# Odd chunks with their halves swapped: 64x64 products over four quarters of the array, and a block-diagonal serial product

## The chip, the cores and the metric

The kernel runs on one core of one Trainium2 chip. The metric is device time in microseconds of one execution of the whole program. The core has a matrix engine (TensorE, PE in the profile; its weight loads are listed as PEld), three engines for elementwise work (VectorE, DVE; ScalarE, ACT; GpSimd, POOL) and SyncE (SP), whose queue issues most of the transfers. TensorE writes its results to PSUM, in banks of 128 partitions by 512 float32; VectorE and ScalarE read them from there.

## What is computed

A hybrid decoder block over 16 meta tokens and 1024 tokens of width 1024: a half-step SwiGLU, then a mixer with two branches, (A) a chunked gated DeltaNet and (B) an RWKV-7 time mixing, then a second half-step SwiGLU. All is float32. The change is in branch B, whose recurrence the reference gives a token at a time:

```python
def _rwkv7_scan(r, w, k, v, a_vec, b_vec):
    def step(state, inp):
        r_t, w_t, k_t, v_t, a_t, b_t = inp
        sa = jnp.einsum('bhvk,bhk->bhv', state, a_t)
        state = state * w_t[:, :, None, :] + sa[..., None] * b_t[:, :, None, :] \
            + v_t[..., None] * k_t[:, :, None, :]
        return state, jnp.einsum('bhvk,bhk->bhv', state, r_t)
    ...
```

B has 16 heads of 64 channels. The kernel takes chunks of 64 tokens, and writes what a chunk does to the state as products of 64x64 matrices.

## The kernel before

The program has three stages: `ffn1`, `middle` and `ffn2`. `middle` works in two segments of 512 tokens (the first has the 16 meta tokens beside them) and, in each, through eight iterations; an iteration handles one head of A and two heads of B, which lie in partitions 0 to 63 and 64 to 127 (`HS`). So there are 16 iterations, with `NCB` = 8 chunks of B in each.

An iteration is made of actions: `new_b` and `new_a` (nine projections of the input with `gates`, 24 matmuls of 128x128 for each block of columns, tile `pp`, and the operands from them), `operands` (products within a chunk, tiles `grb`, `bkt`, `vp`), `inverses` (the triangular inverses in blocks of 32: operands go to DRAM and come back as `Ub`, VectorE solves them, the results go out and return as `Xc` and `Y`), `merge_blocks` (inverses of 64 from those of 32, tiles `iv`), `chains` with `transitions` in front of it (products of the chunks that need the inverse, then the serial part over the chunks), `gates` and `finish`. In the regular case iteration `it` runs `merge_blocks chains`, then `new_b new_a operands inverses` of the next iteration, then `gates finish`. That is the order in which the program is written; the order in which each engine gets its instructions is made by the framework's planner, which goes by priority in the written order, by readiness and by its own estimate of times. The timeline of the trace therefore shows projections of the next iteration between the steps of `chains`.

A 64x64 product takes rows (the partitions of its operands) and columns (the partitions of its result) of the array, a half of each: four quarters. `rows 0 to columns 0` and `1 to 1` are the diagonal ones. In `operands` and `transitions` the 64x64 products go chunk by chunk and half by half:

- `vbp` in `new_b`, L984: 16 products off the diagonal (from half `hp` to half `hx`), into `Vs`.
- `bkt`, L1150: both kinds of `BK` transposed, one to the same half and one to the other: all four quarters, two PSUM banks.
- `vp`, L1167: first `pa` (diagonal) with `pv` (off it), then `pr` with `pk`, both off it. ScalarE copies them to `at`, `vka`, `yb`, `vbk`.
- `transitions`, L1319: six runs of 16 products on the diagonal: `xp` twice (the inverse times `at`, and times `vka`), `mp`, `np`, `rp`, `yp`, each in a bank of its own of the pool `ch`, which has two.
- `chains`, L1397: for each chunk the serial product `b`, two 64x64 matmuls (`mt` times the state `SBs`), then VectorE's update of the state, L1398. After every second chunk comes a chunk of A (tiles `p`, `pq`).

The trace has two records for each float32 matmul, so a run of 16 products is 32 records, and a `b` of one chunk is four. The pool `ch` serves `merge_blocks`, `transitions`, `chains` and `finish`; the pool `mx` serves `new_b` and `operands`, with two banks in the first segment and three in the second.

## Time and profile before

| | |
|---|---|
| Time, median of 3 runs | 3205.22 us (3203.47 to 3205.88) |
| The profiled execution | 3201.6 us, span 3199.8 us |
| TensorE busy | 3064.5 us (96%), 25654 matmul records |
| VectorE, ScalarE, GpSimd busy | 1950.8, 1330.9 and 457.8 us |
| Mean granted TensorE clock | 0.98 |
| first start of `grb` and last start of `bq` in `middle` | 840.6 and 2411.2 us |

The page of the profile gives busy time by engine, the same in 40 slices, the chain of work that ended last, and groups of instructions by line. The span leaves out 1.8 us around it. Matmuls overlap, so the sum of their lengths is not the time that TensorE needs for them; what counts is how far apart they start. A row of the timeline is a stretch of like instructions: start, length from the first start to the last end, engine, line, operation, what it writes and reads, and the count. A bracket tells of idle time before it and what ended it.

### The profile page before, as it was taken

The page shows a single profiled execution, that of the slowest core. Times are in us where ns is not written, and L with a number is a line of the kernel's source. Part 1 is how long each engine was busy: PE and PEld are TensorE (multiplying, and loading weights), DVE is VectorE, ACT ScalarE, POOL GpSimd, SP SyncE. Part 2 cuts the span into 40 slices and gives each one's busy share as a digit, 9 for nine tenths or more (in the row PEclk, how much of TensorE's full clock was granted, in tenths as well). Part 3 has the DMA queues.
Part 4 walks back from the last instruction along what each step waited for, and adds up shares of the span by engine and source line. Part 5 has one row for each costly group of instructions (what it writes and reads, how often), then busy time and mean ns, then how long its engine had stood idle before and what let it go on. Part 6 is the DMA issues. An engine that isn't in the chain of part 4 may idle for free.

```text
span 3199.8 us, 61487 instructions
## 1 busy us (share of the span) xinstructions
PE 3064.5 (96%) x25654; PEld 2578.9 (81%) x25654; DVE 1950.8 (61%) x3628; ACT 1330.9 (42%) x2196; POOL 457.8 (14%) x588
## 2 busy tenths in 40 slices
PE   5999999999899999999999999999999899999998
PEld 5999998998878887888777777777776688887886
DVE  7554444346666776667667777667766755554335
ACT  4222222125545555455565555555544422222114
POOL 4222220000000000000011000011001433322000
PEclk8999999999999999999999999999999999999999
DMA  2222224234122322222332232322255132224323
GB/s 92 93 94 80 80 83 160 77 95 142 60 66 65 81 61 70 69 72 73 92 92 70 73 82 66 79 76 77 76 163 174 64 99 91 80 79 147 109 79 110
DMA packets 256566, 287.16 MB, mean 90 GB/s; under 512 B 168272, under 2 KB 174416, under 8 KB 256288
## 3 DMA queue, kind: packets, MB, share of 16 engines
q1 hardware_dynamic: 252048, 271.42, 28.5%
q0 software_dynamic: 2512, 8.65, 0.7%
q8 instruction: 201, 3.29, 0.4%
q10 hardware_dynamic: 1728, 3.16, 0.3%
q14 instruction: 77, 0.63, 0.1%
HBM read 232.70 MB, written 50.47 MB: 88 GB/s over the span
## 4 chain that ended last, share of the span: by engine, by line
PE 62%; DVE 5%; ACT 3%; DMA 2%; issue 2%; POOL 1%; SPq 0%; DVEq 0%; POOLq 0%; ACTq 0%
PE pp L259 24%; PE pg L422 12%; PE pd L259 7%; PE pwo L259 3%; PE cs L921 2%; PE vp L1167 1%; DMA Xc<-scX 1%; PE b L1397 1%; PE gra L1121 1%; PE grb L1080 1%; PE p L1376 1%; PE bkt L1150 1%; PE pq L1385 1%; DVE w L155 1%; PE iv L1278 1%
## 5 line engine op out<-in xcount | busy, mean ns | idle before, releaser
L259 PE MATMUL pp<-uk,w 128*128 128x264 f32 (+1 forms) x4824 | 987.8, 353 | 3.8 <-DVE gg L1437 3.8
L259 PEld LDWEIGHTS pp<-uk,w 128*128 128x128 f32 x4824 | 751.7, 192 | 122.5 <-issue 21.2
L154 ACT ACTIVATE w<-wraw 128x1024 fp32r<-128x1024 f32 (+2 forms) x332 | 328.5, 990 | 731.7 <-PE pd L259 289.9
L259 PE MATMUL pd<-hd,w 128*128 128x512 f32 (+1 forms) x2640 | 501.0, 352 | 13.2 <-DVE w L155 6.0
L259 PEld LDWEIGHTS pd<-hd,w 128*128 128x128 f32 x2640 | 430.2, 190 | 82.9 <-DVE w L155 8.1
L422 PE MATMUL pg<-bt,w 128*128 128x260 f32 (+1 forms) x2772 | 458.0, 322 | 22.5 <-ACT bt L154 9.4
L422 PEld LDWEIGHTS pg<-bt,w 128*128 128x128 f32 x2772 | 401.5, 190 | 67.6 <-ACT bt L154 10.0
L428 DVE TENSOR_TENSOR c<-c,pg 128x520 f32<-128x520 f32 (+1 forms) x308 | 207.9, 688 | 366.7 <-PE pg L422 301.6
L155 DVE TENSOR_TENSOR w<-wraw,w 128x1024 fp32r<-128x1024 f32 (+2 forms) x332 | 381.9, 1150 | 78.8 <-ACT w L154 72.9
L422 PE MATMUL pg<-b,w 128*128 128x260 f32 (+1 forms) x2376 | 392.3, 321 | 9.2 <-POOL b L155 5.0
L422 PEld LDWEIGHTS pg<-b,w 128*128 128x128 f32 x2376 | 345.7, 190 | 44.2 <-POOL b L155 5.4
L392 POOL TENSOR_TENSOR wrx<-wrx 128x512 f32<-128x512 f32 x44 | 66.6, 1513 | 575.6 <-DVE w22b L155 308.4
L154 ACT ACTIVATE w<-wrx 128x1024 fp32r<-128x1024 f32 (+1 forms) x66 | 60.2, 912 | 180.4 <-PE pg L422 170.0
L1245 DVE TENSOR_TENSOR Xb<-Xb,tb 115x126 f32<-115x126 f32 (+22 forms) x496 | 126.0, 254 | 12.3
L1243 DVE TENSOR_TENSOR tb<-Ub,Xb 115x126 f32<-115x126 f32 (+22 forms) x496 | 125.1, 252 | 11.9 <-DMA Ub<-scr 0.2
L1043 DVE SCALAR_TENSOR_TENSOR acc<-xr,pk,acc 128x528 f32<-128x528 f32 (+1 forms) x144 | 108.7, 755 | 30.7 <-ACT acc L1039 28.6
L539 DVE SCALAR_TENSOR_TENSOR h<-pd,h 128x528 f32<-128x528 f32 (+1 forms) x64 | 44.5, 697 | 119.6 <-PE pd L259 119.6
L539 DVE SCALAR_TENSOR_TENSOR hh<-pd,hh 128x512 f32<-128x512 f32 x64 | 44.1, 689 | 109.9 <-PE pd L259 106.5
L259 PE MATMUL pwo<-uk,w 128*128 128x512 f32 x384 | 99.1, 409 | 6.2 <-ACT rg L922 2.7
L259 PEld LDWEIGHTS pwo<-uk,w 128*128 128x128 f32 x384 | 71.6, 191 | 25.7 <-ACT rg L922 3.5
L839 ACT ACTIVATE sh<-pp,pk 128x528 f32<-128x528 f32 (+1 forms) x54 | 37.2, 690 | 126.9 <-PE pp L259 115.8
L154 ACT ACTIVATE hd<-hr 128x1040 fp32r<-128x1040 f32 (+1 forms) x44 | 45.4, 1061 | 79.1 <-DMA hr<-hid 52.6
(382 smaller groups left out, 3980.2 us busy)
## 6 DMA issues: line engine op xcount, KB each, us to landing
wraw<-in_win SPq DMA_DIRECT2D x150, 512.0 KB
wraw<-in_wgu SPq DMA_DIRECT2D x44, 512.0 KB
wrx<-in_wgu SPq DMA_DIRECT2D x44, 512.0 KB
wraw<-in_wdn SPq DMA_DIRECT2D x48, 320.0 KB
wraw<-in_wdn SPq DMA_DIRECT2D x32, 384.0 KB
hid<-c SPq DMA_DIRECT2D x44, 260.0 KB
hr<-hid SPq DMA_DIRECT2D x22, 520.0 KB
hid<-c SPq DMA_DIRECT2D x44, 256.0 KB
```

The costliest lines, as they stand in the source:

```text
L154: g.nc.scalar.activation(hi, src, AF.Copy)
L155: (eng or g.nc.vector).tensor_tensor(lo, src, hi.bitcast(F32), op=ALU.subtract)
L259: g.nc.tensor.matmul(ps, lhsT=l, rhs=r, start=i == 0, stop=i == n - 1)
L392: nc.gpsimd.tensor_tensor(a22, a21, a22, op=ALU.add)
L422: nc.tensor.matmul(ps[:, c0 : c0 + cn], lhsT=l[:, x, k, :], rhs=r[:, k, y, c0 : c0 + cn], start=i == 0, stop=i == 3 * HK - 1)
L428: nc.vector.tensor_tensor(o, x, y, op=ALU.add)
L539: nc.vector.scalar_tensor_tensor(hv, pd, 0.5, hv, op0=ALU.mult, op1=ALU.add)
L839: nc.scalar.activation(sh[:, 1 : 1 + n], ps, AF.Identity, scale=g.V("mu", i))
L921: nc.tensor.matmul(ps[:, :cn], lhsT=lhsT, rhs=sq[:, c0 : c0 + cn], start=True, stop=True)
L1043: nc.vector.scalar_tensor_tensor(acc[:, :n], xr[:, tap : tap + n], V("convw", ct * 4 + tap), acc[:, :n], op0=ALU.mult, op1=ALU.add)
L1243: nc.vector.tensor_tensor(tv, U[:, i, i + 1 :].unsqueeze(2).to_broadcast([npt, nt, ncc]), X[:, i, 0:ncc].unsqueeze(1).to_broadcast([npt, n ...
L1245: nc.vector.tensor_tensor(X[:, i + 1 :, 0:ncc], X[:, i + 1 :, 0:ncc], tv, op=ALU.add)
```

## The change

For odd chunks the two heads swap halves on the side of the tokens: `tok(i, h)` is the half in which head `h` of chunk `i` has its tokens, `key(i, h)` the other one. A product of an even chunk on diagonal quarters then lies off the diagonal for an odd chunk, and the reverse. A new function `run` issues one or more kinds of products one after another; results of diagonal quarters go to one PSUM bank and those of the others to a second, so that a kind has its even chunks in one bank and its odd ones in the other, four chunks (256 columns) each, and each copy out of PSUM becomes two of half the width. The two kinds of one call share the two banks.

- `new_b`: `vbp` goes through `run`.
- `operands`: `pa` with `pr` in one call, `pk` (`vb`) in another. `pv` moves to `transitions` (`va`). `LT` and `BKt` are held by diagonal and off-diagonal, no longer by kind.
- `inverse_inputs`: the four stores of `LT` become eight, even and odd chunks apart.
- `transitions`: four calls: the inverse times `at` (`px`) with `va`; the inverse times `vka`; `mp` with `rp`; `np` with `yp`. The multiply of `vbk` by `gam` goes from GpSimd to VectorE.
- `g.mt` is a tile of 128x128 for each chunk, allocated once and cleared once, with the two heads' matrices as its diagonal blocks; `b` is one matmul with it.

```diff
--- before.py
+++ after.py
@@ -30,7 +30,7 @@
 NT = NCB + NCA
 NBLK = 4 * NT
 HS = (slice(0, 64), slice(64, 128))
-HX = ((HS[0], HS[1]), (HS[1], HS[0]))
+EO = (slice(0, NCB, 2), slice(1, NCB, 2))
 CDEC = math.exp(-0.5)
 EPS = 1e-6
 NJ = 8
@@ -720,7 +720,9 @@
         g.Y = [ms.tile([P, NT, P], F32, name=f"Y{i}") for i in range(2)]
         g.XA = ms.tile([CB, NCA, 2, 2, 16], F32, name="XA")
         g.Ub = ms.tile([115, 32, 32], F32, name="Ub")
-        for t in (*g.Y, g.XA, g.Ub):
+
+        g.mt = ms.tile([P, NCB, P], F32, name="mt")
+        for t in (*g.Y, g.XA, g.Ub, g.mt):
             nc.gpsimd.memset(t, 0.0)
 
         g.unit = ms.tile([P, CB], F32, name="unit")
@@ -924,6 +926,38 @@
         nc.scalar.activation(out[:, :n], out[:, :n], AF.Exp, scale=-0.5)
     else:
         nc.scalar.activation(out[:, :n], out[:, :n], AF.Exp, scale=-0.5, bias=bias)
+
+
+def tok(i, h):
+
+    return h ^ (i & 1)
+
+
+def key(i, h):
+
+    return 1 - tok(i, h)
+
+
+def run(g, pool, name, *kinds):
+
+
+    ps, out, used = {}, [], [0, 0]
+    for f in kinds:
+        ds = [f(i, 0)[2] ^ f(i, 0)[3] for i in range(2)]
+        at = []
+        for d in ds:
+            if d not in ps:
+                ps[d] = pool.tile([P, 512], F32, name=name, tag=pool.name)
+            at.append(used[d])
+            used[d] += NCB // 2 * CB
+        for i in range(NCB):
+            e, c0 = ds[i & 1], at[i & 1] + i // 2 * CB
+            for h in range(2):
+                l, r, src, dst = f(i, h)
+                assert src ^ dst == e
+                g.nc.tensor.matmul(ps[e][HS[dst], c0 : c0 + CB], lhsT=l, rhs=r, start=True, stop=True)
+        out.append([(ch3(ps[d][:, c0 : c0 + NCB // 2 * CB], CB), cs) for d, c0, cs in zip(ds, at, EO)])
+    return out
 
 
 def new_b(g, it):
@@ -978,12 +1012,9 @@
 
     Vs = q.Vs = st.tile([P, NCB, CB], F32, name="Vs", tag="Vs", bufs=2)
     k = shifted(g, c, 40 + j, 8 + j, "kB")
-    ps = g.mx.tile([P, 512], F32, name="vbp", tag="mx")
-    for i in range(NCB):
-        for hp, hx in HX:
-            nc.tensor.matmul(ps[hx, i * CB : (i + 1) * CB], lhsT=v[hp, off + i * CB : off + (i + 1) * CB],
-                             rhs=g.C("cmat")[hp, hp], start=True, stop=True)
-    nc.scalar.activation(Vs, ch3(ps, CB), AF.Copy)
+    for ps, cs in run(g, g.mx, "vbp", lambda i, h: (v[HS[h], off + i * CB : off + (i + 1) * CB],
+                                                    g.C("cmat")[HS[h], HS[h]], h, key(i, h)))[0]:
+        nc.scalar.activation(Vs[:, cs], ps, AF.Copy)
     if meta:
         ps = g.mx.tile([P, 512], F32, name="vbm", tag="mx")
         nc.tensor.matmul(ps[:16, 0:P], lhsT=v[:, 0:16], rhs=g.C("cmat"), start=True, stop=True)
@@ -1071,16 +1102,17 @@
 
 
 
+
     LT = q.LT = st.tile([P, NCB, 2, P], F32, name="LT", tag="LT", bufs=2)
     for c4 in range(0, NCB, 4):
         ps = [g.mx.tile([P, 512], F32, name="grb", tag="mx") for _ in range(2)]
         for i in range(4):
-            for y in range(2):
-                for hp in HX:
-                    nc.tensor.matmul(ps[y][hp[y], i * P : (i + 1) * P], lhsT=BK[hp[0], c4 + i, y],
-                                     rhs=AR[hp[0], c4 + i].rearrange("p a b -> p (a b)"), start=True, stop=True)
-        for y in range(2):
-            nc.vector.tensor_tensor(LT[:, c4 : c4 + 4, y], ch3(ps[y], P),
+            for d in range(2):
+                for h in range(2):
+                    nc.tensor.matmul(ps[d][HS[h ^ d], i * P : (i + 1) * P], lhsT=BK[HS[h], c4 + i, d ^ (i & 1)],
+                                     rhs=AR[HS[h], c4 + i].rearrange("p a b -> p (a b)"), start=True, stop=True)
+        for d in range(2):
+            nc.vector.tensor_tensor(LT[:, c4 : c4 + 4, d], ch3(ps[d], P),
                                     g.C("mB").unsqueeze(1).to_broadcast([P, 4, P]), op=ALU.mult)
     if meta:
         nc.vector.tensor_copy(g.bkpm[0:64, 0, :], g.bkm[0:64, :])
@@ -1142,40 +1174,36 @@
     inverse_inputs(g, q)
 
     BKt = q.BKt = st.tile([P, NCB, 2, CB], F32, name="BKt", tag="BKt", bufs=2)
-    at = q.at = st.tile([P, NCB, CB], F32, name="at", tag="at")
+    ident = g.C("ident")
     ps = [g.mx.tile([P, 512], F32, name="bkt", tag="mx") for _ in range(2)]
     for i in range(NCB):
-        for y in range(2):
-            for hp in HX:
-                nc.tensor.matmul(ps[y][hp[y], i * CB : (i + 1) * CB], lhsT=BK[hp[0], i, y],
-                                 rhs=g.C("ident")[hp[0], hp[0]], start=True, stop=True)
-    for y in range(2):
-        nc.scalar.activation(BKt[:, :, y], ch3(ps[y], CB), AF.Copy)
+        for d in range(2):
+            for h in range(2):
+                nc.tensor.matmul(ps[d][HS[h ^ d], i * CB : (i + 1) * CB], lhsT=BK[HS[h], i, d ^ (i & 1)],
+                                 rhs=ident[HS[h], HS[h]], start=True, stop=True)
+    for d in range(2):
+        nc.scalar.activation(BKt[:, :, d], ch3(ps[d], CB), AF.Copy)
 
     Vs = q.Vs
-    vka, vbk = (st.tile([P, NCB, CB], F32, name=x, tag=x) for x in ("vka", "vbk"))
-    q.vka, q.vbk = vka, vbk
+    at = q.at = st.tile([P, NCB, CB], F32, name="at", tag="at")
+    vbk = q.vbk = st.tile([P, NCB, CB], F32, name="vbk", tag="vbk")
     yb = q.yb = st.tile([P, FULL], F32, name="yb", tag="yb", bufs=2)
 
-    def kind(name, *ops):
-
-        ps = [g.mx.tile([P, 512], F32, name=name, tag="mx") for _ in ops]
-        for i in range(NCB):
-            for p, op in zip(ps, ops):
-                for hp, hx in HX:
-                    l, r = op(i, hp, hx)
-                    nc.tensor.matmul(p[hp, i * CB : (i + 1) * CB], lhsT=l, rhs=r, start=True, stop=True)
-        return ps
-
-    ident = g.C("ident")
-    pa, pv = kind("vp", lambda i, hp, hx: (AR[hp, i, 0, :], ident[hp, hp]),
-                  lambda i, hp, hx: (LT[hx, i, 1, :CB], Vs[hx, i]))
-    nc.scalar.activation(at, ch3(pa, CB), AF.Copy)
-    nc.scalar.activation(vka, ch3(pv, CB), AF.Copy)
-    pr, pk = kind("vp", lambda i, hp, hx: (Vs[hx, i], LT[hx, i, 1, CB:]),
-                  lambda i, hp, hx: (BKt[hx, i, 1], Vs[hx, i]))
-    nc.scalar.activation(yb, pr, AF.Copy)
-    nc.scalar.activation(vbk, ch3(pk, CB), AF.Copy)
+    def vr(i, h):
+        k = key(i, h)
+        return Vs[HS[k], i], LT[HS[k], i, 1 - (i & 1), CB:], k, h
+
+    def vb(i, h):
+        k = key(i, h)
+        return BKt[HS[k], i, 1 - (i & 1)], Vs[HS[k], i], k, h
+
+    pa, pr = run(g, g.mx, "vp", lambda i, h: (AR[HS[h], i, 0, :], ident[HS[h], HS[h]], h, tok(i, h)), vr)
+    for ps, cs in pa:
+        nc.scalar.activation(at[:, cs], ps, AF.Copy)
+    for ps, cs in pr:
+        nc.scalar.activation(ch3(yb, CB)[:, cs], ps, AF.Copy)
+    for ps, cs in run(g, g.mx, "vp", vb)[0]:
+        nc.scalar.activation(vbk[:, cs], ps, AF.Copy)
     if meta:
         btm = q.btm = st.tile([64, P], F32, name="btm", tag="btm")
         ps = g.mx.tile([P, 512], F32, name="btp", tag="mx")
@@ -1207,7 +1235,8 @@
     sv = scr.rearrange("(t b) r c -> b r t c", b=4)
     for b in range(4):
         sl, lo = slice(32 * b, 32 * b + 32), 32 * (b % 2)
-        nc.sync.dma_start(sv[b][:, 0:NCB], q.LT[sl, :, 0, lo : lo + 32])
+        for e, cs in enumerate(EO):
+            nc.sync.dma_start(sv[b][:, cs], q.LT[sl, cs, e, lo : lo + 32])
     for b in range(4):
         sl = slice(32 * b, 32 * b + 32)
         nc.sync.dma_start(sv[b][:, NCB:], q.UA[sl, :, 32 * b : 32 * b + 32])
@@ -1274,7 +1303,7 @@
     ps = g.ch.tile([P, 512], F32, name="iv1", tag="ch")
     for t in range(NT):
         for o in (0, 64):
-            u12 = LT[o : o + 32, t, 0, 32:64] if t < NCB else UA[o : o + 32, t - NCB, o + 32 : o + 64]
+            u12 = LT[o : o + 32, t, t & 1, 32:64] if t < NCB else UA[o : o + 32, t - NCB, o + 32 : o + 64]
             nc.tensor.matmul(ps[o + 32 : o + 64, t * 32 : t * 32 + 32], lhsT=u12, rhs=nat(Xc[o : o + 32, t]),
                              start=True, stop=True)
     for o in (0, 64):
@@ -1308,30 +1337,47 @@
 
     nc, st = g.nc, g.st
     Y = g.Y[q.it % 2]
-    AR, LT, BKt, vbk, yb = q.AR, q.LT, q.BKt, q.vbk, q.yb
-    flat = lambda t: t.rearrange("p c m -> p (c m)")
-
-    def product(pool, name, op):
-        ps = getattr(g, pool).tile([P, 512], F32, name=name, tag=pool)
-        for i in range(NCB):
-            for hp in HS:
-                l, r = op(i, hp)
-                nc.tensor.matmul(ps[hp, i * CB : (i + 1) * CB], lhsT=l, rhs=r, start=True, stop=True)
-        return ps
-
-    xa, xv = (st.tile([P, NCB, CB], F32, name=x, tag=x) for x in ("xa", "xv"))
-    nc.scalar.activation(flat(xa), product("ch", "xp", lambda i, hp: (Y[hp, i, hp], q.at[hp, i])), AF.Copy)
-    nc.scalar.activation(flat(xv), product("ch", "xp", lambda i, hp: (Y[hp, i, hp], q.vka[hp, i])), AF.Copy)
-    mt = q.mt = st.tile([P, NCB, CB], F32, name="mt", tag="mt")
-    ps = product("ch", "mp", lambda i, hp: (xa[hp, i], BKt[hp, i, 0]))
-    nc.vector.tensor_tensor(mt, ch3(ps, CB), g.unit.unsqueeze(1).to_broadcast([P, NCB, CB]), op=ALU.add)
-    ps = product("ch", "np", lambda i, hp: (BKt[hp, i, 0], xv[hp, i]))
-    nc.vector.tensor_tensor(vbk, ch3(ps, CB), vbk, op=ALU.add)
-    nc.gpsimd.tensor_tensor(vbk, vbk, q.gam.unsqueeze(2).to_broadcast([P, NCB, CB]), op=ALU.mult)
-    ps = product("ch", "rp", lambda i, hp: (xa[hp, i], LT[hp, i, 0, CB:]))
-    nc.vector.tensor_tensor(AR[:, :, 1, :], ch3(ps, CB), AR[:, :, 1, :], op=ALU.add)
-    ps = product("ch", "yp", lambda i, hp: (xv[hp, i], LT[hp, i, 0, CB:]))
-    nc.vector.tensor_tensor(yb, ps, yb, op=ALU.add)
+    AR, LT, BKt, Vs, vbk, yb = q.AR, q.LT, q.BKt, q.Vs, q.vbk, ch3(q.yb, CB)
+    xa, xv, vka = (st.tile([P, NCB, CB], F32, name=x, tag=x) for x in ("xa", "xv", "vka"))
+
+    def solved(r):
+        def f(i, h):
+            t = tok(i, h)
+            return Y[HS[t], i, HS[t]], r[HS[t], i], t, t
+        return f
+
+    def by_tok(l, r):
+        def f(i, h):
+            t = tok(i, h)
+            return l(HS[t], i), r(HS[t], i), t, h
+        return f
+
+    def va(i, h):
+        k = key(i, h)
+        return LT[HS[k], i, 1 - (i & 1), :CB], Vs[HS[k], i], k, 1 - k
+
+    px, pv = run(g, g.ch, "xp", solved(q.at), va)
+    for ps, cs in pv:
+        nc.scalar.activation(vka[:, cs], ps, AF.Copy)
+    for ps, cs in px:
+        nc.scalar.activation(xa[:, cs], ps, AF.Copy)
+    for ps, cs in run(g, g.ch, "xp", solved(vka))[0]:
+        nc.scalar.activation(xv[:, cs], ps, AF.Copy)
+    bt = lambda r, i: BKt[r, i, i & 1]
+    br = lambda r, i: LT[r, i, i & 1, CB:]
+    pm, pr = run(g, g.ch, "mp", by_tok(lambda r, i: xa[r, i], bt), by_tok(lambda r, i: xa[r, i], br))
+    for ps, cs in pm:
+        for hp in HS:
+            nc.vector.tensor_tensor(g.mt[hp, cs, hp], ps[hp], g.unit[hp].unsqueeze(1).to_broadcast([CB, NCB // 2, CB]),
+                                    op=ALU.add)
+    for ps, cs in pr:
+        nc.vector.tensor_tensor(AR[:, cs, 1, :], ps, AR[:, cs, 1, :], op=ALU.add)
+    pn, py = run(g, g.ch, "np", by_tok(bt, lambda r, i: xv[r, i]), by_tok(lambda r, i: xv[r, i], br))
+    for ps, cs in pn:
+        nc.vector.tensor_tensor(vbk[:, cs], ps, vbk[:, cs], op=ALU.add)
+    nc.vector.tensor_tensor(vbk, vbk, q.gam.unsqueeze(2).to_broadcast([P, NCB, CB]), op=ALU.mult)
+    for ps, cs in py:
+        nc.vector.tensor_tensor(yb[:, cs], ps, yb[:, cs], op=ALU.add)
 
 
 def chains(g, q):
@@ -1393,8 +1439,7 @@
     nc.gpsimd.tensor_copy(SBs[:, 0], SB)
     for i in range(NCB):
         ps = pt("b1")
-        for hp in HS:
-            nc.tensor.matmul(ps[hp, :CB], lhsT=q.mt[hp, i], rhs=SBs[hp, i], start=True, stop=True)
+        nc.tensor.matmul(ps[:, :CB], lhsT=g.mt[:, i], rhs=SBs[:, i], start=True, stop=True)
         nc.vector.scalar_tensor_tensor(SBs[:, i + 1], ps[:, :CB], q.gam[:, i : i + 1], q.vbk[:, i],
                                        op0=ALU.mult, op1=ALU.add)
         if i % 2 == 0:
```

## Prediction

> **What bounds the kernel now.** I read the page first: busy shares, the slices, the chain that ended last.
>
> ```profile
> span 3199.8 us, 61487 instructions
> PE 3064.5 (96%) x25654; PEld 2578.9 (81%) x25654; DVE 1950.8 (61%) x3628; ACT 1330.9 (42%) x2196; POOL 457.8 (14%) x588
> PE   5999999999899999999999999999999899999998
> PE 62%; DVE 5%; ACT 3%; DMA 2%; issue 2%; POOL 1%; SPq 0%; DVEq 0%; POOLq 0%; ACTq 0%
> ```
>
> TensorE is busy 96% of the span and in every slice but the first; the chain runs mostly over it. The change lies in the middle stage, so the next view is the table of stretches: one iteration of the first segment, one of the second.
>
> ```profile
> 1044.00:1144.00 100.00, 94.65 (x1067) 79.56 (x1065) 66.76 (x162) 50.03 (x97) 8.40 (x25) 0.98 0.27 72
> 2049.00:2141.00 92.00, 89.51 (x956) 68.63 (x952) 66.37 (x151) 49.94 (x89) 8.72 (x18) 1.00 0.29 77
> ```
>
> Columns: length, then busy time of PE, PEld, DVE, ACT and POOL with instruction counts, granted clock, DMA. TensorE fills 94.7 of 100 and 89.5 of 92 us; VectorE has a quarter free, ScalarE half. The list of TensorE's waits tells what the rest is.
>
> ```profile
> PE iv L1278 <- DMA Xc<-scX: 14.4, 7, 2.8
> PE vbp L984 <- DVE vB L840: 7.2, 3, 4.9
> PE vp L1167 <- ACT BKt L1153: 2.6, 8, 0.6
> PE np L1319 <- ACT xv L1324: 1.4, 5, 0.3
> ```
>
> (Total, times, longest.) The largest wait that comes again is 14.4 us in seven iterations, for the inverses' blocks that come back by DMA. The products that the change touches hardly wait. So the middle lasts as long as TensorE's instructions take one after another, and what is to be priced is TensorE time.
>
> **A product on two quarters and on four.** A 64x64 product is one matmul in the program and two records in the trace. From the timeline, one iteration's products on the diagonal quarters alone:
>
> ```profile
> 1930.17 1.15 PE L1319 MATMUL xp<-vka,Y 64*64 64x64 f32 x32
> 1931.20 1.15 PE L1319 MATMUL mp<-BKt,xa 64*64 64x64 f32 x32
> 1932.63 1.15 PE L1319 MATMUL np<-xv,BKt 64*64 64x64 f32 x32 [0.28 <-ACT xv L1324]
> 1934.77 1.15 PE L1319 MATMUL rp<-LT,xa 64*64 64x64 f32 x32
> 1935.75 1.10 PE L1319 MATMUL yp<-LT,xv 64*64 64x64 f32 x32
> 1936.71 0.33 PE L1397 MATMUL b<-SBs,mt 64*64 64x64 f32 x4
> ```
>
> One record lasts 0.22, so 32 records start within 1.15 - 0.22 = 0.93 us: 29 ns each. For four quarters there are two places. The transposes `bkt` use all four (the stretch from 1257, those instructions alone), and so do the first two kinds of `vp` where they run well:
>
> ```profile
> 1257.00:1259.00 2.00, 1.44 (x64) 1.30 (x64) 0.37 (x1) 1.00 0.18 26
> 1874.86 0.22 PE L1167 MATMUL vp<-Vs,LT 64*64 64x64 f32 x1
> 1874.86 0.22 PE L1167 MATMUL vp<-ck,AR 64*64 64x64 f32 x1
> 1874.87 0.22 PE L1167 MATMUL vp<-Vs,LT 64*64 64x64 f32 x1
> 1874.87 0.22 PE L1167 MATMUL vp<-ck,AR 64*64 64x64 f32 x1
> 1874.92 0.22 PE L1167 MATMUL vp<-Vs,LT 64*64 64x64 f32 x1
> ```
>
> 64 records of `bkt` start within 1.44 - 0.22 = 1.22 us, 19 ns each. In the steady part four start within 0.01 us and the next four 0.06 us later, 15 ns each. A quarter takes one record in 58 ns whatever the others do; `bkt` loses 0.29 us over its steady rate (64 x 14.5 ns = 0.93) because the second of its two PSUM banks comes free later, and its records on that bank trail.
>
> Here a rule speaks against the change. The Trainium skill, page "TensorE: Matmul & The Clock Gate", section "Part 3: Packing small matmuls — row/col tiling", says that a weight load overlaps running matmuls only where it targets other rows of the array. By it, two quarters that share rows would take turns, four would give no more than two, and the products would gain nothing; the rows of `bkt` and `vp` above disagree.
>
> **The change part by part, per iteration (16 of them).** There are eleven products of 16 matmuls before and after; what moves is which quarters meet in one run. From the index functions in the diff: `vbp`, `pa` with `pr`, `pk`, `mp` with `rp`, `np` with `yp` alternate over four quarters. But `solved` reads rows `t` and writes rows `t`: `px` and the second `xp` stay on the diagonal, and `va`, emitted after `px`, stays off it. Those three keep the rate of two quarters. In us:
> - before: `vbp` 0.93; `pa` with `pv` 1.22 (as `bkt`); `pr` with `pk`, both off the diagonal, 1.86; six of `transitions` 5.58. Sum 9.59.
> - after, at 19 ns a record: `vbp` 0.61, `pa`+`pr` 1.22, `pk` 0.61, `px`+`va` 1.86, `xv` 0.93, `mp`+`rp` 1.22, `np`+`yp` 1.22. Sum 7.67, 1.9 less.
> - after, at 15 ns and with `va` starting under the end of `px`: 0.51 + 0.98 + 0.51 + 1.72 + 0.93 + 0.98 + 0.98 = 6.61, 3.0 less.
>
> I take 2.4, half way, since some runs will find their second bank late and others not: 38 us over 16 iterations. Low end: if every run has its even chunks first and the odd ones after, two quarters work at a time throughout and only `pa`, which loses its partner, changes: -0.6 an iteration, a loss of 10 us. High end 49.
>
> **The serial product.** `b` goes from two 64x64 matmuls to one 128x128, 128 times. Timeline, both segments:
>
> ```profile
> 1109.05 1.36 PE L259 MATMUL pp<-uk,w 128*128 128x264 f32 x9
> 1116.92 0.39 PE L259 MATMUL pp<-uk,w 128*128 128x264 f32 x1
> 1127.13 0.89 PE L259 MATMUL pp<-uk,w 128*128 128x264 f32 x5
> 1127.86 0.38 PE L1376 MATMUL p<-SA,kq 128*128 128x128 f32 x2
> 1128.00 0.73 PE L259 MATMUL pp<-uk,w 128*128 128x264 f32 x4
> 1636.08 1.03 PE L895 MATMUL tkp<-ck,c 128*128 128x16 f32 x8 [1.22 <-DVE c L881]
> 1940.35 0.48 PE L259 MATMUL pp<-uk,w 128*128 128x512 f32 x1
> 1940.76 0.33 PE L1397 MATMUL b<-SBs,mt 64*64 64x64 f32 x4
> 1941.02 0.97 PE L259 MATMUL pp<-uk,w 128*128 128x512 f32 x3
> ```
>
> A projection matmul of 512 columns adds (0.97 - 0.48) / 2 = 0.24. From the `pp` ahead of `b` to the `pp` behind it are 0.67, so `b` between projections costs 0.43. A full-array product: `p` is followed by the next `pp` after 0.14; the whole stretch from 1127.13 to 1128.00 is 0.87, less five short projections of 0.12 ((1.36 - 0.39) / 8) it is 0.27, the first projection's start behind `b` included; `tkp`, full array with only 16 columns, needs (1.03 - 0.26) / 7 = 0.11 a record, 0.22 a product. I take 0.22, the one in the middle: 0.21 saved, 128 times, 27 us. Ends: 0.43 - 0.14 = 0.29 gives 37; a `b` that follows a product and not a projection (1936.71 to 1936.97 is 0.26) saves only 0.04, 5 us if all were such. The step's own delay grows from 0.33 to about 0.11 + 0.26 = 0.37; VectorE already waits for `b`, and projections stand between the steps, so the 0.04 x 128 = 5 us are covered; without that cover they come on top.
>
> **What is added.**
>
> ```profile
> L1124 DVE TENSOR_TENSOR UA<-gra,E 128x256 f32<-128x256 f32 x32 | 13.5, 421 | 6.4 <-PE gra L1121 5.8
> L1327 DVE TENSOR_TENSOR mt<-mp,unit 128x512 f32<-128x512 f32 x16 | 11.0, 687 | 12.5 <-PE mp L1319 12.5
> L1330 POOL TENSOR_TENSOR vbk<-vbk,gam 128x512 f32<-128x512 f32 x16 | 19.0, 1187 | 159.7 <-DVE vbk L1329 159.7
> L1323 ACT ACTIVATE xa<-xp 128x512 f32<-128x512 f32 x16 | 9.6, 597 | 3.5 <-PE xp L1319 3.4
> ```
>
> VectorE: four operations of 0.69 become ten halves of 0.42, and the multiply by `gam` (0.69 here, 1.19 on POOL) joins: 4.9 against 2.8, 2.1 us more. ScalarE: seven copies of 0.60 become fourteen of perhaps 0.42, 1.7 more. Both hide under TensorE, since these engines have 25 and 42 us an iteration free; uncovered they are 34 and 27 us in all. The added clear of `mt` on POOL is one of 1024 columns before the stage's first product and hides under the last projections of `ffn1`.
>
> Each run now holds both `ch` banks until all its halves are read, where before one bank was filled while the other was emptied. So TensorE waits four times an iteration for 2 to 6 such operations, 0.8 to 2.5 us, with the chain's `b` and `p` behind it on the same queue. The cover is projections: 9 x 24 an iteration at 0.24, which the planner places into waits that it sees. I count two more interruptions of the projections an iteration at 0.43 - 0.22 = 0.21 each: 7 us lost. Uncovered, four waits of 1.5 us are 96 us.
>
> SP issues eight stores of `LT` for four:
>
> ```profile
> 1871.27 1.80 SPq L1210 DMA_DIRECT2D scr<-LT  x4
> 1873.18 2.65 SPq L1213 DMA_DIRECT2D scr<-UA  x4
> ```
>
> That is 1.8 us more, ahead of the stores of `UA`, the loads of `Ub` and the next weights on that queue. The weights are fetched one tile ahead and hide it. The inverses are later by up to 1.8 us; the second segment shows no wait for them and has some slack, the first waits 2 us in each of seven iterations already, so there this delay and the shorter `vp` work turn into waiting: about 1 us x 7 = 7 us lost, 7 x 3.5 = 25 at most.
>
> **Sum.** 38 + 27 - 7 - 7 = 51. The profiled execution took 3201.6 us, so 3151; the median of the runs shown is 3.6 higher, and on its scale I forecast 3155.
>
> **Rivals.**
> 1. The products gain nothing: the banks come free so far apart that the halves run two quarters at a time (`bkt`'s late bank speaks for it, its 19 ns against it), or quarters that share rows take turns. Left are 27 - 14 = 13 us, with the low end of the products near zero: 3192; with half of the products' gain 3175.
> 2. Everything fits: 49 + 37 and no losses: 3119. For it: VectorE and ScalarE have room. Against it: the wait for `Xc` is there already.
> 3. Slower: the runs that hold both `ch` banks leave TensorE idle. From 51 / 16 = 3.2 us idle an iteration on, the gain is gone; four uncovered waits of 1.5 us give 3155 + 16 x 6 = 3251. For it: the first run of `transitions` now stands ahead of a copy, a product, a copy again. Against it: `np` waited for `xv` 1.4 us in all.
> 4. The change does not do what it says and its costs meet its gains: no change, 3205.
>
> **How the numbers follow.** Forecast (3130 to 3172) 0.60; rival 1 0.20, three quarters of it faster by over 0.2%; rival 2 0.10; rival 3 0.07; rival 4 0.03. 0.2% is 6.4 us, about what a measurement of this kernel can tell from no change. Faster: 0.60 + 0.15 + 0.10 + a little of the rest = 0.86; same 0.07; slower 0.07. The range from 3117 to 3192 takes in most of rivals 1 and 2 and leaves out rival 3.
>
> **What the profile will show.** Right: `vbp`, `mp` with `rp` and `np` with `yp` as runs of 32 and 64 records that start within 0.5 to 0.6 and 1.0 to 1.2 us; `b` with two records, 128x128, and 0.2 us between the projections around it; the iteration of the second segment at 88 to 89 us; `px` and `xv` still at 0.93. Wrong: waits of TensorE for `mt`, `vbk`, `xa` or `xv` of over a microsecond, `Xc` waits above 30 us in all, or VectorE above 80% with TensorE below 93%. What would upset the forecast most is a new order from the planner in which the projections are used up before the runs need them.

## The result and the profile after

| kernel | median, us | runs | ratio to before, 95% interval |
|---|---|---|---|
| before | 3204.34 | 4 | |
| changed | 3176.49 (3172.09 to 3179.78) | 4 | 0.9914, 0.9897 to 0.9931 |
| changed, second time (below) | 3178.90 (3173.06 to 3181.99) | 5 | 0.9928, 0.9916 to 0.9941 |

The change gains 28 us where 50 were forecast; 3176 lies 4 us above the forecast's likeliest case (3130 to 3172) and inside its whole range (3117 to 3192). The profiled execution took 3179.03 us, 22.6 less than the one before, and the readings below are of these two.

Page of the changed kernel: span, busy shares, chain by engine. Then the table of stretches, one iteration of the second segment from `iv` to `iv` (length, busy time of PE, PEld, DVE, ACT, POOL with counts, granted clock, DMA). Then TensorE's waits (total, times, longest).

```profile
span 3177.2 us, 61363 instructions
PE 3048.8 (96%) x25398; PEld 2563.7 (81%) x25398; DVE 1972.4 (62%) x3740; ACT 1336.5 (42%) x2308; POOL 436.2 (14%) x573
PE 62%; DVE 5%; ACT 3%; DMA 3%; issue 1%; POOL 0%; SPq 0%; DVEq 0%; POOLq 0%; ACTq 0%
```

```profile
2080.20:2171.70 91.50, 91.03 (x946) 69.65 (x945) 69.77 (x161) 50.23 (x95) 7.78 (x18) 1.00 0.30 79
```

```profile
PE iv L1307 <- DMA Xc<-scX: 15.8, 7, 3.0
PE np L958 <- DVE AR L1374: 6.0, 3, 3.5
```

TensorE is the bound as before: 96%, at a granted clock of 1.00 in this stretch. The mean of four iterations here went from 91.35 to 90.10 us; in the first segment from 103.3 to 102.5. The wait for `Xc` grew by 1.4 us, and three waits of `np` for VectorE are new. From the first `grb` to the last `bq` the middle takes 1560.5 us, 10 less than before; the other 12 us show behind the last `bq`, mostly because only 225 of the 384 records of the output projection (`pwo`) are left there, where 272 were. That is work moved ahead and not work saved, so the gain is read from the products and not from the stages.

To see where TensorE's time went, I give each of its matmuls in the trace the time from its start to the start of the next one (an idle stretch goes to the matmul ahead of it) and add up by product, us over the whole run. All kernels of the next section stand in the same table. "chain" is `p` and `pq`; "transitions" had six products before and has seven since, `va` having left `vp`.

| product | before | b alone | products alone | changed | two quarters | both edits | va first |
|---|---|---|---|---|---|---|---|
| vbp | 18.1 | 18.1 | 10.7 | 10.7 | 16.9 | 10.4 | 10.4 |
| vp | 64.8 | 65.1 | 49.6 | 50.3 | 54.6 | 44.4 | 49.1 |
| transitions | 104.5 | 100.3 | 103.0 | 103.4 | 106.4 | 100.9 | 84.4 |
| b | 31.4 | 31.0 | 29.1 | 32.6 | 31.9 | 26.5 | 28.5 |
| chain | 77.7 | 73.5 | 82.7 | 79.4 | 77.5 | 80.5 | 79.0 |
| grb | 51.5 | 50.1 | 55.8 | 56.9 | 55.0 | 54.0 | 53.1 |
| pp | 968.9 | 964.6 | 975.5 | 971.6 | 978.2 | 973.8 | 991.0 |
| all other | 1856.3 | 1862.9 | 1844.6 | 1845.7 | 1840.2 | 1845.1 | 1845.8 |
| sum | 3173.2 | 3165.6 | 3151.0 | 3150.6 | 3160.7 | 3135.6 | 3141.3 |

The first three rows are the forecast's "products": 187.4 before, 164.4 after, so 23 us and not 38. `b` costs as much as before. Three runs of products in the changed kernel, from TensorE's timeline (start, length to the last end, count; a row is a group of like instructions, and rows in between are left out):

```profile
1882.73 0.69 PE L958 MATMUL vbp<-ck,vB 64*64 64x64 f32 x32
1914.56 0.63 PE L958 MATMUL mp<-BKt,xa 64*64 64x64 f32 x16
1915.02 0.63 PE L958 MATMUL mp<-LT,xa 64*64 64x64 f32 x14
1915.48 0.68 PE L958 MATMUL mp<-BKt,xa 64*64 64x64 f32 x16
1916.00 0.63 PE L958 MATMUL mp<-LT,xa 64*64 64x64 f32 x18
1919.14 0.73 PE L958 MATMUL np<-xv,BKt 64*64 64x64 f32 x31
1919.71 0.66 PE L958 MATMUL np<-LT,xv 64*64 64x64 f32 x30
```

`vbp`: 32 records start within 0.69 - 0.22 = 0.47 us where two quarters took 0.93. `np` with `yp`: 64 start within 1.0 us here, and within 1.26 in seven of the 16 iterations. But `mp` with `rp` runs the even halves of both products first and then the odd ones, 1.9 us: two quarters at a time. And the chain's steps stand among other products than before:

```profile
1934.66 0.43 PE L1112 MATMUL grb<-AR,BK 64*64 64x128 f32 x2
1935.02 0.43 PE L1442 MATMUL b<-SBs,mt 128*128 128x64 f32 x2
1935.38 0.87 PE L1112 MATMUL grb<-AR,BK 64*64 64x128 f32 x12
```

The next iteration's `grb` now lies between the steps; before, it began after `bq` in the second segment. The planner made a new order: 24 of the 128 `b` stand between two projections, where 45 stood.

### The profile page after: what moved, and what is told of

Same layout as the page of the kernel before. It is cut to its first block, busy times and chain, and to the rows that moved or that the text cites. A ratio compares the mean times of both kernels' runs of the same rounds, so it can differ in the third digit from the quotient of the medians.

```text
span 3177.2 us, 61363 instructions
## 1 busy us (share of the span) xinstructions
PE 3048.8 (96%) x25398; PEld 2563.7 (81%) x25398; DVE 1972.4 (62%) x3740; ACT 1336.5 (42%) x2308; POOL 436.2 (14%) x573
## 4 chain that ended last, share of the span: by engine, by line
PE 62%; DVE 5%; ACT 3%; DMA 3%; issue 1%; POOL 0%; SPq 0%; DVEq 0%; POOLq 0%; ACTq 0%
PE pp L259 23%; PE pg L422 12%; PE pd L259 7%; PE pwo L259 2%; PE cs L923 2%; PE grb L1112 1%; DMA Xc<-scX 1%; PE b L1442 1%; PE xp L958 1%; PE vp L958 1%; PE gra L1153 1%; PE bkt L1182 1%; PE np L958 1%; PE pq L1431 1%; DVE w L155 1%
## 5 line engine op out<-in xcount | busy, mean ns | idle before, releaser
L154 ACT ACTIVATE hd<-hr 128x1040 fp32r<-128x1040 f32 (+1 forms) x44 | 45.4, 1061 | 79.4 <-DMA hr<-hid 52.9
```

Source lines behind the costliest of these rows:

```text
L154: g.nc.scalar.activation(hi, src, AF.Copy)
```

## The experiments

Ratios are to the kernel before, run beside each on the same chip; the experiments ran on three chips, so they are compared with each other by these ratios. The diffs are shortened: `...` and comments stand for what is left out.

**The two parts apart.** The products and `b` each alone. For `b` alone:

```diff
+        g.mt = ms.tile([P, NCB, P], F32, name="mt")      # cleared once
-    nc.vector.tensor_tensor(mt, ch3(ps, CB), g.unit..., op=ALU.add)
+    for hp in HS:
+        nc.vector.tensor_tensor(g.mt[hp, :, hp], ch3(ps, CB)[hp], g.unit[hp]..., op=ALU.add)
-        for hp in HS:
-            nc.tensor.matmul(ps[hp, :CB], lhsT=q.mt[hp, i], rhs=SBs[hp, i], start=True, stop=True)
+        nc.tensor.matmul(ps[:, :CB], lhsT=g.mt[:, i], rhs=SBs[:, i], start=True, stop=True)
```

> The kernel before with the serial product alone changed: mt is one 128x128 block-diagonal tile, b one matmul, the products stay as they were. Theory A: half of the 128 products b wait for ScalarE's copy of pq, which reads the PSUM bank that this b writes; the row of the forecast (0.43 us between projections) was one of these, and its cost is the wait. Such a b stays at 0.40; the other half, which follows the product p, goes from 0.36 to 0.17 (both from the timelines of before and after). That is 64 x 0.19 = 12 us, so 3192, a ratio of 0.996. Theory B, the forecast's: every b saves 0.21, 27 us: 3177, 0.9916. Theory C: the planner gives it all back: within 3 us of before.

Measured 3184.13 (3182.35 to 3195.34), ratio 0.9957 (0.9943 to 0.9972): 14 us, near theory A's 12. The profiled execution was one of the two slowest of six, 3194.05, so its column in the table shows less of the gain. TensorE's timeline of this kernel:

```profile
1937.51 0.48 PE L259 MATMUL pp<-uk,w 128*128 128x512 f32 x1
1937.90 0.43 PE L1398 MATMUL b<-SBs,mt 128*128 128x64 f32 x2
1938.14 0.94 PE L259 MATMUL pp<-uk,w 128*128 128x512 f32 x3
1938.92 0.33 PE L1398 MATMUL b<-SBs,mt 128*128 128x64 f32 x2
1939.09 0.44 PE L1378 MATMUL p<-SA,kq 128*128 128x128 f32 x2
```

The first `b` sits between projections that start 0.63 apart; in the kernel before these were 0.67 (1940.35 to 1941.02 in the prediction). The second goes from projection to `p` in 0.40; before, the median of 31 such places was 0.58. So a `b` of the second kind saves 0.18, and one of the first kind 0.04.

```diff
-        nc.tensor.matmul(ps[:, :CB], lhsT=g.mt[:, i], rhs=SBs[:, i], start=True, stop=True)
+        for hp in HS:
+            nc.tensor.matmul(ps[hp, :CB], lhsT=g.mt[hp, i, hp], rhs=SBs[hp, i], start=True, stop=True)
```

> The changed kernel with b as two 64x64 matmuls on the diagonal blocks of its mt; all the runs of products stay changed. Theory A: the runs themselves take 20 us less (176.8 to 156.6 in the two traces), and with b worth 12 of the 28 us of the whole change, 16 are left to them: 3188, a ratio of 0.995. Theory B, the forecast's sum without b: 38 - 7 - 7 = 24 us: 3180, 0.9925. If b is worth nothing, this run is as fast as the changed kernel, 0.9914.

Measured 3177.17, ratio 0.9922 (0.9910 to 0.9934). That is theory B's number, and the whole gain of the change as far as the intervals can tell: on top of the products the single `b` adds nothing that can be measured, though alone it gave 14 us. The timeline of this kernel shows what a `b` in two parts finds there:

```profile
1938.63 0.44 PE L1112 MATMUL grb<-AR,BK 64*64 64x128 f32 x4
1938.84 0.27 PE L1443 MATMUL b<-SBs,mt 64*64 64x64 f32 x2
1938.89 0.29 PE L1112 MATMUL grb<-AR,BK 64*64 64x128 f32 x2
1938.95 0.23 PE L1443 MATMUL b<-SBs,mt 64*64 64x64 f32 x2
1939.01 0.39 PE L1112 MATMUL grb<-AR,BK 64*64 64x128 f32 x6
```

Among 64x64 `grb` it costs little: from the last `grb` ahead of one part to the `grb` behind it 0.10 us at the median, and 0.21 over both parts, with two records of `grb` between them (18 products). A single 128x128 `b` in that place takes 0.56 (16 times in the changed kernel). 16 x 0.35 = 6 us lost there, an estimate from these medians, eat what the other places gain: 20 places between a projection and `p` at 0.40 and not 0.59 make 4 us, and the 24 between two projections some 2.

**Four quarters or two.**

```diff
-        for i in range(NCB):
+        for i in (*range(0, NCB, 2), *range(1, NCB, 2)):
             e, c0 = ds[i & 1], at[i & 1] + i // 2 * CB
```

> The changed kernel with the matmuls of each run of products emitted in another order: first those of the even chunks, then those of the odd ones, so that at any time only two quarters of the array have work. Same products, halves, banks and b. Theory A: the gain of the change is four quarters at once in vbp, in pa with pr and in np with yp; without it their 8 + 15 us in the trace (vbp 18.1 to 10.7, vp 64.8 to 49.6 of which the moved va is part) and the 10 us of np with yp come back, some 20 us of the 28: 3196, a ratio of 0.997. Theory B: the gain comes from fewer stops and from b, and the order within a run matters little: as the changed kernel, 0.9914. The planner may also place the rest otherwise, by some 5 us.

Measured 3188.18, ratio 0.9962 (0.9950 to 0.9975), near theory A's 0.997: 11 to 15 us given back, and the order of matmuls within the runs is all that was edited. The table has 13.5 of it in the products' rows (`vbp`, `vp`, transitions). In TensorE's timeline the same `vbp` lasts 0.98 and not 0.69, with the odd part starting under the end of the even part:

```profile
1890.70 0.98 PE L958 MATMUL vbp<-ck,vB 64*64 64x64 f32 x32
```

**The wait inside b.** The forecast's row for `b` between projections, here as the changed kernel has it, all engines:

```profile
2105.30 0.19 PEld L259 LDWEIGHTS pp<-uk,w 128*128 128x128 f32 x1
2105.39 0.28 ACT L1435 ACTIVATE kq<-pq 128x128 f32<-128x128 f32 x1 [0.58 <-PE pq L1431]
2105.72 0.30 PEld L1442 LDWEIGHTS b<-SBs,mt 128*128 128x128 f32 x2 [0.22 <-ACT kq L1435]
2105.72 0.43 PE L1442 MATMUL b<-SBs,mt 128*128 128x64 f32 x2
```

`b`'s weights are not loaded under the projection: the load waits until ScalarE's copy of `pq` ends (2105.67), because `pq` was in the bank that `b` takes in the pool of two. The place that the forecast's row is from, in the kernel before, has the same wait; the copy ends at 1940.69:

```profile
1940.41 0.28 ACT L1389 ACTIVATE kq<-pq 128x128 f32<-128x128 f32 x1 [0.58 <-PE pq L1385]
1940.76 0.20 PEld L1397 LDWEIGHTS b<-SBs,mt 64*64 64x64 f32 x4 [0.24 <-ACT kq L1389]
```

The wait isn't everywhere: the places that have it have one projection between `p` and `b`. Where more work stands there, the copy is done before `b`'s turn. One such place of the kernel before, and one of the changed kernel, behind `np`:

```profile
1134.36 0.93 PE L259 MATMUL pp<-uk,w 128*128 128x512 f32 x3
1135.22 0.33 PE L1397 MATMUL b<-SBs,mt 64*64 64x64 f32 x4
1135.48 0.73 PE L259 MATMUL pp<-uk,w 128*128 128x512 f32 x2
2100.26 1.68 PE L259 MATMUL pp<-uk,w 128*128 128x512 f32 x6
2101.78 0.33 PE L1442 MATMUL b<-SBs,mt 128*128 128x64 f32 x2
2101.92 1.18 PE L259 MATMUL pp<-uk,w 128*128 128x512 f32 x4
```

From the projection ahead to the one behind it is 0.58 us with the two-part `b` (0.58 to 0.59 in 14 of its 45 places) and 0.37 with the single one (0.37 to 0.38 in 7 of 24). So without the wait the new shape saves the 0.21 us of the forecast; with it, 0.67 against 0.63 (25 and 15 places), it saves 0.04.

Two edits take the wait away. The first gave `b` another pool:

```diff
-        ps = pt("b1")
+        ps = g.mx.tile([P, 512], F32, name="b1", tag="mx")
```

> The changed kernel with b's result in a bank of pool mx and not of ch, so that it isn't the bank that the copy of pq reads. Theory A: the b behind p and one projection waits for that copy, with its weights not loaded ahead; without the wait the pair of projections around it start 0.15 and not 0.40 us further apart than projections do, 64 x 0.25 = 16 us: 3160, a ratio of 0.986. Rival: the wait was covered by nothing else than the chain's own step, the next product p waits longer instead, or the products in mx get their banks later: the same as the changed kernel, 0.9914, or slower.

Measured 3675.12, ratio 1.1484 (1.1469 to 1.1500). It tells nothing on the wait: the planner's order fell apart. In the second segment the next iteration's `grb` starts 35 us after the first `bq` (in the changed kernel 4 to 10 us ahead of it), and TensorE waits for the inverses. The rival had "or slower", but not this size. This kernel's waits, and an iteration in its table of stretches:

```profile
PE iv L1307 <- DMA Xc<-scX: 272.1, 14, 30.5
```

```profile
2240.40:2362.10 121.70, 99.02 (x940) 79.08 (x940) 69.35 (x158) 50.75 (x95) 5.14 (x16) 0.84 0.22 59
```

The second edit leaves the pools as they are and puts `p3` into `pq`'s bank, so that `b` finds the other one:

```diff
-        p3 = pt("p3")
-        nc.tensor.matmul(p3[:, :P], lhsT=ktl[:, i, :], rhs=vn, start=True, stop=True)
+        p3 = pq[:, 256 : 256 + P]
+        nc.tensor.matmul(p3, lhsT=ktl[:, i, :], rhs=vn, start=True, stop=True)
```

> The changed kernel with the product p3 in the free half of pq's bank, so that the pool ch turns over five banks a chunk pair and not six: b behind p3 gets the bank that ScalarE's copy of vn has left long ago, and no longer the one that the copy of pq still reads. Unlike the run that moved b to pool mx it adds no order between the chain and the next iteration. Theory A: the waiting b falls from 0.40 to about 0.15 us between projections, 64 x 0.25 = 16 us: 3160, a ratio of 0.986. Rival: the wait for the copy of pq moves to the next b, or the state's update waits no less and TensorE loses the time elsewhere: 0.9914 or slower.

Measured 3167.81, ratio 0.9898 (0.9883 to 0.9913): 5 to 10 us below the changed kernel's two results, a third to two thirds of theory A's 16. (The interval overlaps the first of them, 0.9897 to 0.9931, and lies under the second.) The wait itself is gone, in the timeline of all engines:

```profile
1916.47 0.39 PE L1433 MATMUL pq<-vn,ktl 128*128 128x128 f32 x2
1916.59 0.30 PEld L1442 LDWEIGHTS b<-SBs,mt 128*128 128x128 f32 x2
1916.70 0.33 PE L1442 MATMUL b<-SBs,mt 128*128 128x64 f32 x2
1916.84 0.95 PE L259 MATMUL pp<-uk,w 128*128 128x512 f32 x3
```

`b` follows the products directly, its weights load 0.11 ahead, and the next projection starts 0.14 behind it. Of the places between two projections none is left at 0.63 (15 of 24 in the changed kernel). The same edit in the kernel before, where `b` is in two parts:

> The kernel before with the one edit of p3 in pq's bank; products and b as they were. Theory A: b's place between projections, 0.665 us from the projection ahead to the one behind in 39 of 45 cases, is for the most part the wait for the copy of pq, in the kernel before as in the changed one. Without it about 0.2 us go in some 50 places, 10 us: 3190, a ratio of 0.997. Theory B: two 64x64 matmuls between projections cost that much by their size alone, as the forecast took it: no change, 1.000.

Measured 3189.35, ratio 0.9965 (0.9952 to 0.9977), theory A's: the wait was there all along, and taking it away gives 11 us. But theory B has a part in it: the 14 places left between two projections, now without the wait, still take 0.58 to 0.59 with the two-part `b`. (The 39 cases of that text are the 25 at 0.67, which wait, and the 14 at 0.58 to 0.59, which don't.)

Next, the version with the edits of `mp` and of `p3` together (its run with the single `b` follows below), with `b` in two parts again:

```diff
         ps = pt("b1")
-        nc.tensor.matmul(ps[:, :CB], lhsT=g.mt[:, i], rhs=SBs[:, i], start=True, stop=True)
+        for hp in HS:
+            nc.tensor.matmul(ps[hp, :CB], lhsT=g.mt[hp, i, hp], rhs=SBs[hp, i], start=True, stop=True)
```

> The version with mp ahead of xv and p3 in pq's bank, with b as two 64x64 matmuls again. In the changed kernel the single b gained nothing, since 41 of the 128 two-part b stand between two grb, same size, at 0.10 us from the grb ahead to the one behind, and the single b costs 0.56 there (16 times). Theory A: what the single b is worth depends on its neighbours; with p3 in pq's bank it mostly follows pq, 128x128, directly (25 times with a projection behind it, 19 times with grb), and there two 64x64 matmuls bring a change of size at each end: 0.2 us lost in some 45 places, 9 us: 3172, a ratio of 0.9912. Theory B: the form of b is worth nothing in any order: 0.9884, as the version with both edits.

(The 41 stretches of `b` in that text include halves of one product; 18 products had `grb` on both sides.) Measured 3181.31, ratio 0.9937 (0.9924 to 0.9951), against 0.9884 for the version with the single `b` (below): the form of `b` is worth 17 us there and was worth nothing in the changed kernel. From `pq` to the projection behind `b` it is 0.47 us in two parts and 0.25 in one (30 places, 6 us); from a projection to `p` 0.59 and 0.40 (18 places), between two projections 0.59 and 0.37 (11 places), another 6. The rest of the 17 us is not traced.

**The late bank of mp.**

```diff
-    for ps, cs in run(g, g.ch, "xp", solved(vka))[0]:      # both lines move behind the additions to mt and AR
-        nc.scalar.activation(xv[:, cs], ps, AF.Copy)
```

> The changed kernel with the run of mp and rp ahead of the second run xp (xv) in transitions, so that its second bank isn't held by the copies of xv. Theory A: in the changed kernel the 64 records of mp and rp start within 2.0 us, evens first, since the odd half's bank is late; with both banks free they start within 1.0 to 1.2 us, as np with yp do, 0.8 x 16 = 13 us: 3163, a ratio of 0.987. The price is that np with yp comes sooner behind xv and may lose as much. Theory B: the late bank only moves to another run, no net change: 0.9914.

Measured 3177.63, ratio 0.9933 (0.9921 to 0.9946): no gain, theory B's. TensorE's timeline shows to whom the bank moved:

```profile
1912.25 0.52 PE L958 MATMUL mp<-BKt,xa 64*64 64x64 f32 x12
1913.38 0.62 PE L958 MATMUL mp<-BKt,xa 64*64 64x64 f32 x14 [0.38 <-ACT vka L1361]
```

The odd half waits for the copy of `vka` instead of `xv`, and in 15 of the 16 iterations the 64 records start within 1.8 to 2.7 us, no better than before. With the edit of the wait inside `b`:

> The two edits of mp ahead of xv and of p3 in pq's bank together. If each gives what its theory says and they add up, 13 + 16 = 29 us under the changed kernel: 3147, a ratio of 0.982. If they share the cover that the projections give, less than the sum.

Measured 3163.22, ratio 0.9884 (0.9871 to 0.9898): the lowest of all, 10 to 15 us under the changed kernel and not 29. The edit of `mp` alone gave nothing, and the interval overlaps that of the edit of `p3` alone, so that it gives something here is not shown. Next, with the bank of `va` freed early too:

```diff
-    px, pv = run(g, g.ch, "xp", solved(q.at), va)
+    pv, px = run(g, g.ch, "xp", va, solved(q.at))
```

> The version with both edits, and in transitions the products of va ahead of those of px. With mp ahead of xv alone the odd half of mp and rp waited for the bank of va, whose copy came last. Theory A: with va first its copy is done while px runs, mp and rp find both banks free, and their 64 records start within 1.0 to 1.2 us, not 1.9 to 2.0: 0.8 x 16 = 13 us under the version with both edits, 3150, a ratio of 0.984. Theory B: va first only delays px and xa, on which mp waits, and the bank is late again or TensorE is filled otherwise: 0.988.

Measured 3170.91, ratio 0.9907 (0.9893 to 0.9920), 7 us slower than without this edit by the ratios, with intervals that overlap by a little. Yet theory A's mechanism is there. TensorE's timeline, and its waits:

```profile
1910.65 0.69 PE L958 MATMUL mp<-BKt,xa 64*64 64x64 f32 x32
1911.16 0.65 PE L958 MATMUL mp<-LT,xa 64*64 64x64 f32 x32
1911.74 2.59 PE L259 MATMUL pp<-uk,w 128*128 128x512 f32 x10
1915.43 1.15 PE L958 MATMUL xp<-vka,Y 64*64 64x64 f32 x32 [1.09 <-DVE AR L1372]
```

```profile
PE xp L958 <- DVE AR L1372: 12.9, 14, 1.1
PE b L1442 <- DVE yb L1380: 5.1, 7, 1.1
```

The 64 records start within 1.0 us, and the transitions fall from 100.9 to 84.4 us in the table. But the run holds both banks until VectorE has added four halves of `mt` and two of `AR`. That is 2.5 us of work, about what the ten projections cover (2.59), but VectorE begins it 1.3 us after the run's end, behind another operation (`kq`):

```profile
1912.51 0.69 DVE L1082 TENSOR_TENSOR kq<-acc,sg 128x512 f32<-128x512 f32 x1 [1.37 <-ACT sg L926]
1913.12 1.72 DVE L1369 TENSOR_TENSOR mt<-mp,unit 64x256 f32<-64x256 f32 x4
1914.86 0.76 DVE L1372 TENSOR_TENSOR AR<-mp,AR 128x256 f32<-128x256 f32 x2
```

TensorE waits 18 us in all, nearly all of which stands in the row `pp` (the matmul ahead).

**grb out of the chain.**

```diff
+                after.enter_context(g.tc.issue_after(g.bq.ins))   # grb behind the last bq
```

> The changed kernel with the 64x64 matmuls of grb held behind the last bq of the iteration before, where the trace of before has them (in the changed kernel's second segment they stand between the steps of the chain). Theory A: each change between 64x64 and 128x128 products costs 0.2 to 0.37 us there, and taking grb out of the chain gives back 1 to 1.5 us in each of about 8 iterations, 8 to 12 us: 3165 to 3168, a ratio of 0.988. Theory B: the interleaving costs nothing net, since what follows grb (LT, the inverses) is late when grb is: the same as the changed kernel, 0.9914, or slower.

Measured 3351.77, ratio 1.0471 (1.0457 to 1.0484). Neither theory foresaw this size. TensorE's waits and one iteration:

```profile
PE vbp L958 <- DVE Xb L1277: 46.7, 6, 8.5
```

```profile
2017.70:2127.20 109.50, 96.77 (x941) 74.41 (x940) 67.06 (x158) 51.34 (x95) 5.47 (x16) 0.89 0.25 64
```

In the second segment `grb` starts 1.6 us after the first `bq`, as it did before the change (1.4), but everything else was laid out anew: VectorE has the inverses ahead of what `vbp` needs, the inverses last 40 us from VectorE's first instruction to its last where they lasted 28, and TensorE runs dry. So it does not answer what the interleaving costs net; that stays open, and of the table's rows only `grb` (+5) and the chain (+2) speak for a cost.

**The changed kernel again,** beside the last runs.

> The changed kernel itself, unedited, on the chip of the three runs beside it, so that they can be set against it directly: 0.9914 of the kernel before, within its interval of 0.990 to 0.993.

Measured 3178.90, ratio 0.9928 (0.9916 to 0.9941). The version with both edits (0.9871 to 0.9898) lies under it.

## Why the prediction was half right

- *What bounds.* Right: TensorE's time, instruction after instruction, 96% on both sides.
- *Products, 38 us.* The mechanism was right, the size was not: 23 us by the table. `vbp` (0.47 us) and `np` with `yp` (1.0 to 1.26 in most iterations) came out about as written, and so did `pa` with `pr` in the first segment (1.21); in the second these two ran one behind the other (1.87). `mp` with `rp` was mis-sized: 1.9 us for the forecast 1.0 to 1.2, since its second bank was late, as rival 1 had it for all runs; 0.8 us over 16 iterations are 13 of the 15 us that are missing. `pk` needed 0.73 where it ran in one piece, not 0.5 to 0.6. That the concurrency counts is shown by the order alone (two quarters: 11 to 15 us back), and that the late bank made the 1.9 by the run with `va` first (1.0 with both banks free). (The high end of this term is 16 x 3.0 = 48, not 49.) The Trainium skill's rule on the page "TensorE: Matmul & The Clock Gate", section "Part 3: Packing small matmuls — row/col tiling", that a weight load overlaps only with work on other rows, would have left `vbp` at 0.93 us as the prediction worked it out: this case's 0.47 disagrees.
- *Serial product, 27 us.* This step failed. Its row of 0.43 us was of a `b` that waits for a bank, which the new shape shortens by 0.04 and not 0.21, and the price was then put on all 128. Where no wait stands the 0.21 was right (0.58 against 0.37), and once the wait is gone the shape is worth 17 us (the version with both edits). Alone `b` gave 14 us; on top of the products nothing that could be measured, since the new order puts 16 of them between 64x64 `grb`, at 0.56 us where the two-part `b` had cost 0.21. The prediction held the row for one of `b` between projections without asking what had ended the wait ahead of its weight load.
- *Losses, 14 us.* The products without `b` gave 25 us, and the forecast's sum without `b` was 24, but not by its parts: the products gave 14 less, the wait for `Xc` cost 1.4 and not 7, and the rows "all other" gained 12 that nobody had forecast while `grb`, chain and `pp` lost 16. So the agreement of 25 with 24 is luck. So is that of the measured 3176 with rival 1's 3175, which had `b`'s 27 us in it whole. What made the 12 is not traced; 9 of them stand at the matmuls `bon` (19.9 us before, 10.6 with the products alone).
- *VectorE and ScalarE.* Sizes right, from the groups of the changed kernel:

```profile
L1371 DVE TENSOR_TENSOR mt<-mp,unit 64x256 f32<-64x256 f32 x64 | 27.0, 421 | 9.6 <-PE mp L958 8.9
L1363 ACT ACTIVATE xa<-xp 128x256 f32<-128x256 f32 x32 | 10.5, 380 | 12.2 <-PE xp L958 12.2
```

  Halves of 0.42 and 0.38 us, hidden but for the 6.0 us of `np` waiting for `AR`. What they would cost uncovered is rival 3, and a part of it showed once the run of `mp` was made fast: 18 us of waits.
- *The signs to look for.* The iteration was to be 88 to 89 us and is 90.1. `b` was to add 0.2 us between projections and adds 0.39 (0.63 less the projection's 0.24) in 15 of 24 places. Of the signs of being wrong none came as named; the three waits of `np` for `AR`, the longest 3.5 us, are of their kind. The upset named last, a new order of the planner, is what happened: `grb` fills the chain's gaps where projections had stood.

## What to carry to other kernels

Before a row of the timeline becomes the price of an instruction, look at what ended the wait ahead of its weight load: here the new shape saved 0.21 us where nothing was waited for and 0.04 where a bank was late, and taking away the reuse of that bank was worth about as much (11 us in the kernel before) as the new shape alone (14). The price of a small matmul is set by its neighbours (0.10 us for a 64x64 among 64x64, 0.56 for a 128x128 in their place), so two edits to one queue need not add up, and each must be run with the other. When all quarters of the array work on one run, its banks are all held at once, and the engine that empties them can become the next wait (18 us with `va` first).

## What the hardware showed that was not expected

- Four quarters take one product each at a time whether or not they share rows: 32 records of 64x64 started within 0.47 us, 64 within 1.0, and 0.93 us for 32 was the rate of two quarters.
- While the wait for a bank stood, `b`'s weights were not loaded ahead (the load and the first matmul both start at 2105.72, behind the copy's end at 2105.67). The projections around a single `b` start 0.37 to 0.38 us apart without the wait and 0.63 with it.
- Where TensorE ran dry, the granted clock fell too: 1.00 in an iteration of the changed kernel, 0.89 in one with `grb` held back, 0.84 in one with `b` in the other pool. So a wait there may cost more than its own length; no run separates the two.
